# Placing loads and stores in one transfer queue of a streaming-encoder step

## The chip, the cores and the metric

The kernel runs on one core of one Trainium2 chip. The metric is the device time of one execution in microseconds. Five engines work side by side, each through its own list of instructions: TensorE (PE, with its weight loads shown apart as PEld), VectorE (DVE), ScalarE (ACT), GpSimd (POOL) and SyncE (SP). SP computes nothing here. It issues every transfer of the kernel.

## The reference, cut to what matters

One layer of an encoder with two attention branches, for 2048 new frames of one stream ("prompt") and 16 new frames of each of 8 running streams ("sample", 128 rows in all, with caches of 512 past positions):

```
h, gate = rms_norm(x) * (1 + scale) + shift, gate      # scale, shift, gate = c @ w_ada + b_ada
qa ka va za qb kb vb zb ga gb = split(h @ w_in)        # 4 heads A of 2x64, 8 heads B of 64, two gates of 1024
qa, ka = rope(qa), rope(ka)
oa = (softmax(qa1 ka1') - lam * softmax(qa2 ka2')) va  # a query sees keys of its 64-frame chunk and before
ob = stick_breaking(qb kb') vb                         # a running product over the keys, last key first
oa = rms_norm(oa) * 0.8
y  = (sigmoid(ga) * ((oa*silu(za)) @ w_a) + sigmoid(gb) * ((ob*silu(zb)) @ w_b)) @ w_out
out = rms_norm(x + gate * y)
```

The new rows of ka, va, kb and vb are outputs as well, and so are stored row by row while the projection runs.

## The kernel before

**Stages.** A first stage makes the modulated h, turns it so that features lie on partitions, splits it into a float16 high and low part, and writes it to DRAM (hT_d, 512 KB for each tile of 128 rows). The middle stage works through eight units. A unit is one head of the softmax branch (kind 0) or two heads of the stick-breaking branch (kind 1), in turn. For each unit it projects 17 tiles of h, the sample tile first, and runs causal attention for the 16 prompt tiles. A last stage does the sample attention against the caches, the branch products, the merge and the output. Between the stages o (attention output), z and the two gates g pass through DRAM (o_d, z_d, g_d).

**One step of the projection** (`project`, L405) is one tile t of one unit. Its pieces are given out one at a time: pieces 0 to 11 are two products each, 24 products over 512 columns that add up q, k, v and z in one PSUM bank (`mm`, L423 to L426: high with high, high with low, low with high, for 8 blocks of features). The piece after the last product copies the bank out on ACT to `pr` (L440), rotates q and k on POOL for kind 0 (`rot`, L459 to L464, with the small table `rope`), splits v, k and q into float16 pairs, and issues the stores: new k (L474), new v (L475), z (L477). Units 1 to 7 also carry columns of the gates, in 24 more products (L493) into the bank tagged "t", copied to one half of the buffer `gts` (L496) and stored (L497).

**Where h comes from.** `fetch_h` (L400) loads a tile of hT_d into one of three 512 KB buffers `hs`, in turn (L403). `projection` (L847) calls it for the next step at piece 2 of the running one (`H_AT`). The first tiles are at hand from the first stage.

**Attention.** `scores` multiplies q with k (L628, L629). Kind 0 takes the softmax, kind 1 a scan on DVE (L605) and a product on POOL (L611). `turn` then makes float16 pairs (L561, L562, or L289 with L294) and a transposing transfer turns them (L569) into `wt`, five buffers. Two rounds later `pv` multiplies `wt` with v (L676 to L681); ACT or DVE scales the result into `o` (L657, L663) and `store` sends it to o_d (L670).

**What sets the order.** All pieces of all projection steps stand in one list, `line`. In each round n of the middle stage (L1202) a stretch of that list, the score pieces of tile n and the pv pieces of round n - 2 are mixed by `interleave` (L91); `position` keeps the projection about five steps ahead. This gives the order in which the program is written. The framework's scheduler then decides the order on each engine: with `schedule_with_timeline_sim=True` it takes instructions on a time line of its own, and may write a transfer down earlier or later among SP's entries than it was given. On the chip each engine runs its list in that order. SP's list is one queue: an entry that has to wait holds all entries behind it. A transfer's completion is counted on one of eight semaphores, in turn.

`load` is `nc.sync.dma_start`; stores go through it too. `tc.add_manual_dep(..., NOSYNC)` binds only the written order, and adds no wait on the chip.

Of the kernel before, what the change touches and what calls it, by code (L numbers as in the profile page):

```python
# [25 lines left out]
P = 128  # L26
D = 1024
KT = D // P
# [20 lines left out]
S_TILES = 13  # L49
S_PERIOD = 6  # L50
H_AT = 2
Q_BUFS = 6
TR_AFTER = 5
LEAD = 5.0
# [55 lines left out]
def layer_kernel(ctx: ExitStack, tc: tile.TileContext, a: dict):  # L110
    nc = tc.nc
    V, S, G, T = nc.vector, nc.scalar, nc.gpsimd, nc.tensor
    load = nc.sync.dma_start
# [3 lines left out]
    def act(**kw):  # L117

        i = S.activation(**kw)  # L119
        if last_table[0] is not None:  # L120
            tc.add_manual_dep(i.ins, last_table[0].ins.name, NOSYNC, reason="table order")
        last_table[0] = i
        return i

    x_p = a["x_prompt"][0]
    x_s = a["x_sample"].rearrange("b s d -> (b s) d")
# [271 lines left out]
    at_hand, ahead, fetched = {}, {}, []  # L398

    def fetch_h(u, t):  # L400
        ahead[u, t] = hs[len(fetched) % 3].bitcast(F16).rearrange("p (f k n) -> p f k n", f=2, n=P)
        fetched.append(t)
        load(out=ahead[u, t], in_=hT_d[t // 4][:, t % 4, :, :, :])  # L403

    def project(U, t):  # L405

# [4 lines left out]
        def start():  # L411
            if t in at_hand:
                box["h"] = at_hand.pop(t)
            else:
                if (U["u"], t) not in ahead:
                    fetch_h(U["u"], t)
                box["h"] = ahead.pop((U["u"], t))
            box["p"] = bank("mm")
            if kind == 0:
                box["r"] = stg.tile([P, 96], F32, tag="rope", name="rope")  # L420
                load(out=box["r"], in_=a["shapes"][:, t * 96 : t * 96 + 96])

        def mm(n):  # L423
            hi, wi = ((0, 0), (0, 1), (1, 0))[n % 3]
            k = n // 3
            T.matmul(box["p"], box["h"][:, hi, k, :], U["w"][k][:, wi, :], start=(n == 0), stop=(n == 3 * KT - 1))  # L426

        def piece(n):
            if n == 0:
# [6 lines left out]
        def finish():  # L436
            p, s2, s = box["p"], sc[:, 2:3], sq[:, 0:1]
            pr = stg.tile([P, 512], F32, tag="pr", name="pr", bufs=3)
            first = P * kind
            S.activation(out=pr[:, first:512], in_=p[:, first:512], func=AF.Identity, scale=sc[:, 1:2])  # L440

            qb = qbuf[t % len(qbuf)]
            k16 = stg.tile([P, 2, 2, 64], F16, tag="k16", name="k16")
            vt = kvp.tile([P, 2, 2, 64], F16, tag="v", name="v", bufs=V_BUFS)

            def halves(dst, src, scale):
                src = src.rearrange("p (c d) -> p c d", d=64)
                split(dst[:, :, 0, :], dst[:, :, 1, :], src, scale, S)

            def query(src, scale):  # L450
                src = src.rearrange("p (c d) -> p c d", d=64)
                S.activation(out=qb[:, 0, :, :, :], in_=src.unsqueeze(2).to_broadcast([P, 2, 2, 64]), func=AF.Identity, scale=scale)
                V.scalar_tensor_tensor(out=qb[:, 1, :, 0, :], in0=src, scalar=scale, in1=qb[:, 0, :, 0, :], op0=ALU.mult, op1=ALU.subtract)
            if kind == 0:
                cosT, sinT = box["r"][:, 0:32], box["r"][:, 32:96]
                x4 = pr[:, 0:256].rearrange("p (c f d) -> p c f d", c=4, f=2)
                rot = stg.tile([P, 256], F32, tag="rot", name="rot")
                r2 = stg.tile([P, 256], F32, tag="r2", name="r2", bufs=1)
                G.tensor_tensor(out=rot.rearrange("p (c f d) -> p c f d", c=4, f=2), in0=x4,  # L459
                                in1=cosT.unsqueeze(1).unsqueeze(1).to_broadcast([P, 4, 2, 32]), op=ALU.mult)  # L460
                G.tensor_tensor(out=r2.rearrange("p (c f d) -> p c f d", c=4, f=2), in0=x4[:, :, ::-1, :],
                                in1=sinT.rearrange("p (f d) -> p f d", f=2).unsqueeze(1).to_broadcast([P, 4, 2, 32]),
                                op=ALU.mult)
                G.tensor_tensor(out=rot, in0=rot, in1=r2, op=ALU.add)  # L464
# [9 lines left out]
            load(out=out_rows(nk, t, h * P, P), in_=rot[:, 128:256])  # L474
            load(out=out_rows(nv, t, h * P, P), in_=pr[:, 256:384])  # L475
            ui = (h + 4 * kind) * P
            load(out=z_d[t][:, ui : ui + P], in_=pr[:, 384:512])  # L477
# [8 lines left out]
        def gate_piece(n):  # L486

            if n == 0:
                box["g"] = bank("t")
            for j in range(per * n, per * n + per):  # L490
                hi, wi = ((0, 0), (0, 1), (1, 0))[j % 3]
                k = j // 3
                T.matmul(box["g"][:, 0:gw], box["h"][:, hi, k, :], U["wg"][k // per][:, k % per, wi, :], start=(j == 0), stop=(j == 3 * KT - 1))  # L493
            if per * n + per == 3 * KT:
                gt = gts[:, t % 2 * 512 : t % 2 * 512 + 512]
                S.activation(out=gt[:, 0:gw], in_=box["g"][:, 0:gw], func=AF.Identity, scale=sc[:, 6:7])  # L496
                load(out=g_d[t][:, g0 : g0 + gw], in_=gt[:, 0:gw])  # L497
# [168 lines left out]
    def store(U, t, o):  # L666
        ui = (U["h"] + 4 * U["kind"]) * P
        if U["kind"] == 0:
            sum_squares(o, P, osums[:, t, U["h"] : U["h"] + 1])
        load(out=o_d[t][:, ui : ui + P], in_=o)  # L670

    def pv_block(job, seg, po, wj, vt, first, last):

# [173 lines left out]
    def projection(m):  # L847
# [337 lines left out]
    def early_work():  # L1185
# [202 lines left out]
```

## Time and profile before

| what | value |
| --- | --- |
| runs | 2426.85 us median of 3 (2415.17 to 2428.43) |
| profiled execution | 2416.58 us; its span, first to last instruction, 2414.4 us |
| mean granted clock of TensorE | 0.954 |
| loads of h (L403) | 130, of 512 KB each |
| turning transfers (L569) into wt | 288 |
| rope loads (L421) | 68 |
| stores of k, v, z (L474, L475, L477) | 136 of each |
| stores of o (L670), of gates (L497) | 136, 119 |
| transfers that SP issues in all | 1279 plain, 332 turning |

How to read it: the span is that of one execution taken by the hardware profiler, and the runs are timed without it. A row "A <- B: 10.0, 5, 3.0" of the waits says that A stood idle 10.0 us before its instruction, in 5 pauses, the longest 3.0 us, until B let it go. A row of the time line has the start and the length in us, the engine and line, the operation, what it writes and reads, and, in brackets, the pause ahead of it. "SPq" marks SP's list; its issue of a transfer is shown as a span there, and the transfer itself lands later.

### The profile page before, as it was taken

What the parts mean: (1) busy time and instruction counts of PE and PEld (TensorE: products, weight loads), DVE (VectorE), ACT (ScalarE), POOL (GpSimd) and SP (SyncE); (2) the same over time, 40 slices, a digit from 0 to 9 for tenths busy, and PEclk for the clock granted to TensorE, in tenths of its full rate; (3) what the DMA queues carried; (4) which work ended last, traced back from release to release, by engine and by line L of the source; (5) the groups of instructions that cost most, each with busy time, mean ns of one, the idle gap of its engine ahead of it and who ended that gap; (6) DMA issues with size and microseconds to landing.
All of it is one profiled execution on the core that took longest, in us unless ns stands there. A gap on an engine that the chain in (4) does not pass through costs nothing. (4 is left out here: it accounts for less than half of the span.)

```text
span 2414.4 us, 45136 instructions
## 1 busy us (share of the span) xinstructions
PE 2129.1 (88%) x16366; PEld 1247.2 (52%) x16366; DVE 1746.9 (72%) x3668; ACT 1664.5 (69%) x3264; POOL 754.2 (31%) x607
## 2 busy tenths in 40 slices
PE   5879998899999899899988898999995688888998
PEld 2435665565665556556555555655553344444443
DVE  4868778886676788667778976657778767777754
ACT  3658788886777878566777876665777667666652
POOL 1733023453102346220124542102334333332322
PEclk7989999999999999999999999999997889999999
DMA  9668969985886998577588866756688999998521
GB/s 334 215 204 205 215 161 217 221 182 134 189 219 168 211 195 177 129 174 177 134 215 175 182 154 149 186 129 158 154 179 184 274 240 254 252 244 214 158 104 53
DMA packets 854000, 453.91 MB, mean 188 GB/s; under 512 B 539050, under 2 KB 806362, under 8 KB 853264
## 3 DMA queue, kind: packets, MB, share of 16 engines
q1 hardware_dynamic: 853776, 451.03, 75.3%
q8 instruction: 128, 2.10, 0.4%
q14 instruction: 96, 0.79, 0.1%
HBM read 249.80 MB, written 73.44 MB: 134 GB/s over the span
## 5 line engine op out<-in xcount | busy, mean ns | idle before, releaser
L611 POOL TENSOR_TENSOR sc_p<-sc_p,sc_n 128x127 f32<-128x127 f32 (+7 forms) x192 | 318.9, 1664 | 755.4 <-DVE sc_n L605 736.6
L426 PEld LDWEIGHTS <-hs 128*128 128x128 f16 x3120 | 278.9, 99 | 320.5 <-DMA hs<-hT_d 58.4
L426 PE MATMUL ps_mm<-wa,hs 128*128 128x512 f16 x1590 | 405.9, 388 | 28.3 <-DMA hs<-hT_d 28.3
L426 PE MATMUL ps_mm<-wb,hs 128*128 128x512 f16 x1530 | 391.2, 385 | 22.6 <-DMA hs<-hT_d 19.1
L493 PEld LDWEIGHTS <-hs 128*128 128x128 f16 x2856 | 275.5, 98 | 93.9 <-DVE qst L521 4.3
L605 DVE TENSOR_TENSOR_SCAN sc_n<-ps_s,sc_n,zero_t 128x512 f32<-128x512 f32 x192 | 245.6, 1279 | 48.6 <-ACT ps_s L119 42.4
L562 DVE TENSOR_TENSOR sc_n<-sc_p,sc_n 128x128 f16<-128x128 f32 (+7 forms) x192 | 232.1, 1214 | 27.8 <-ACT sc_n L561 27.3
L628 PE MATMUL ps_s<-k,qst 128*128 128x512 f16 (+3 forms) x640 | 224.8, 352 | 29.0 <-DVE sc_n L605 24.5
L493 PE MATMUL ps_t<-wb,hs 128*128 128x256 f16 (+1 forms) x1734 | 241.0, 292 | 0.7 <-DVE qst L521 0.6
L119 ACT ACTIVATE sc_p<-ps_s,usc 128x512 f32<-128x512 f32 (+3 forms) x320 | 206.1, 644 | 36.1 <-PE ps_s L629 17.8
L629 PE MATMUL ps_s<-k,qst 128*128 128x512 f16 (+3 forms) x640 | 224.1, 352 | 0.0
L119 ACT ACTIVATE ps_s<-ps_s,usc 128x512 f32<-128x512 f32 (+3 forms) x328 | 201.4, 614 | 0.0
L561 ACT CAST sc_n<-sc_p 128x128 f16<-128x128 f32 (+7 forms) x192 | 156.1, 818 | 64.3 <-POOL sc_p L611 63.9
L680 PE MATMUL ps_o<-v,wt 128*128 128x128 f16 x1088 | 156.7, 226 | 41.0 <-DMA wt<-sc_n 40.7
L1309 PE MATMUL ps_o<-wo,wb 128*128 128x512 f16 x816 | 188.9, 385 | 0.7 <-ACT wb L1127 0.7
L1268 PE MATMUL ps_mm<-wa,wb 128*128 128x512 f16 x612 | 166.4, 403 | 20.5 <-DVE sy L225 14.2
L459 POOL TENSOR_TENSOR rot<-pr,rope 128x256 f32<-128x256 f32 x68 | 62.5, 919 | 381.6 <-ACT pr L440 299.3
L547 DVE TENSOR_SCALAR_CACHE_REDUCE sc_p<-ps_s,usc 128x512 f32<-128x512 f32 (+3 forms) x160 | 106.6, 666 | 82.0 <-PE ps_s L629 58.7
L680 PEld LDWEIGHTS <-wt 128*128 128x128 f16 x1088 | 104.5, 102 | 93.3 <-DMA wt<-sc_n 53.2
L493 PE MATMUL ps_t<-wa,hs 128*128 128x256 f16 (+1 forms) x1122 | 148.7, 282 | 1.5 <-DVE qst L521 1.5
L547 DVE TENSOR_SCALAR_CACHE_REDUCE sc_n<-ps_s,usc 128x512 f32<-128x512 f32 (+3 forms) x160 | 106.6, 666 | 53.6 <-PE ps_s L629 28.4
L681 PE MATMUL ps_o<-v,wt 128*128 128x64 f16 x1088 | 144.8, 198 | 0.0
(338 smaller groups left out, 4530.7 us busy)
## 6 DMA issues: line engine op xcount, KB each, us to landing
hs<-hT_d SPq DMA_DIRECT2D x130, 512.0 KB, 4.3
wb<-g_d SPq DMA_DIRECT2D x26, 512.0 KB, 5.1
out_dram<-pr SPq DMA_DIRECT2D x204, 64.0 KB, 2.3
g_d<-gt SPq DMA_DIRECT2D x102, 128.0 KB, 3.8
wide<-in_w_ada_dram SPq DMA_DIRECT2D x12, 1024.0 KB, 8.9
wa<-in_w_in_dram SPq DMA_DIRECT2D x34, 256.0 KB, 6.2
z_d<-pr SPq DMA_DIRECT2D x136, 64.0 KB, 1.7
o_d<-o SPq DMA_DIRECT2D x136, 64.0 KB, 3.0
```

The source lines that it names most:

```text
L119: i = S.activation(**kw)
L426: T.matmul(box["p"], box["h"][:, hi, k, :], U["w"][k][:, wi, :], start=(n == 0), stop=(n == 3 * KT - 1))
L493: T.matmul(box["g"][:, 0:gw], box["h"][:, hi, k, :], U["wg"][k // per][:, k % per, wi, :], start=(j == 0), stop=(j == 3 * KT - 1))
L547: V.tensor_scalar(out=dst[:, lo : lo + n], in0=p[:, 0:n], scalar1=sc_pos, scalar2=None, op0=ALU.mult, op1=ALU.max, accum_out=job["mx"][:, ...
L562: V.tensor_tensor(out=lo, in0=src, in1=hi, op=ALU.subtract)
L605: V.tensor_tensor_scan(out=dst[:, lo : lo + n][:, ::-1], data0=src[:, 0:n][:, ::-1], data1=zero_t[:, 0:1].to_broadcast([P, n]), initial=fi ...
L611: G.tensor_tensor(out=p[:, 0:m], in0=p[:, 0:m], in1=n[:, 1 : m + 1], op=ALU.mult)
L628: T.matmul(p[:, 0:n], qst[:, c, :], kk[:, c, 0:n], start=True, stop=False)
L629: T.matmul(p[:, 0:n], qst[:, 2 + c, :], kk[:, c, 0:n], start=False, stop=not diag)
L680: T.matmul(po[:, c * P : (c + 1) * P], wt[:, wj, :], vt[:, c, :, :], start=first, stop=False)
L1268: T.matmul(pb, st["u"][:, ui * 8 + br * 4 + k, :], wb[br * 4 + k // 2 * 2 + j][:, wi, k % 2, :], start=(n == 0), stop=(n == 11))
L1309: T.matmul(po, st["y"][:, yi * 8 + k, :], wo[j * 4 + k // 2][:, wi, k % 2, :], start=(n == 0), stop=(n == 3 * KT - 1))
```

## The change

Four things change, all in the middle stage, and no arithmetic. Line numbers are those of the kernel before.

- Each product of the projection is remembered as `last_mm`. The loads of h (L403) and of rope (L421) get an order edge to the last product given so far. So in SP's list they may not be written ahead of that product's place in the scheduler's time line: the load of h for the next step behind the fourth product of the running step, the rope load behind the last product of the step before.
- The stores at L474, L475, L477, L497 and L670 are no longer given at once. They are put in a list, which is given out at piece 5 of the next projection step (`STORE_AT`), behind its tenth product, with the same order edge. When the projection has ended, the list is given out once a round.
- The halves of `gts` alternate by the count of gate tiles, not by the parity of t. (Tile 16 and tile 0, which follow each other, had the same half.)
- Before the middle stage stores are given at once, as they were.

```diff
+STORE_AT = 5
...
+    last_mm = [None]
+
+    def not_ahead(i):
+
+        if last_mm[0] is not None:
+            tc.add_manual_dep(i.ins, last_mm[0].ins.name, NOSYNC, reason="place in the queue")
+
+    stores, late_stores = [], [False]
+
+    def store_late(**kw):
+
+        if late_stores[0]:
+            stores.append(kw)
+        else:
+            load(**kw)
+
+    def give_stores(n):
+        for kw in stores[:n]:
+            not_ahead(load(**kw))
+        del stores[:n]
...
-        load(out=ahead[u, t], in_=hT_d[t // 4][:, t % 4, :, :, :])
+        not_ahead(load(out=ahead[u, t], in_=hT_d[t // 4][:, t % 4, :, :, :]))
...
-                load(out=box["r"], in_=a["shapes"][:, t * 96 : t * 96 + 96])
+                not_ahead(load(out=box["r"], in_=a["shapes"][:, t * 96 : t * 96 + 96]))
...
-            T.matmul(box["p"], box["h"][:, hi, k, :], U["w"][k][:, wi, :], start=(n == 0), stop=(n == 3 * KT - 1))
+            last_mm[0] = T.matmul(box["p"], box["h"][:, hi, k, :], U["w"][k][:, wi, :], start=(n == 0), stop=(n == 3 * KT - 1))
...
-            load(out=out_rows(nk, t, h * P, P), in_=rot[:, 128:256])
-            load(out=out_rows(nv, t, h * P, P), in_=pr[:, 256:384])
+            store_late(out=out_rows(nk, t, h * P, P), in_=rot[:, 128:256])
+            store_late(out=out_rows(nv, t, h * P, P), in_=pr[:, 256:384])
...
-                gt = gts[:, t % 2 * 512 : t % 2 * 512 + 512]
+                j = len(gated) % 2 * 512
+                gated.append(t)
+                gt = gts[:, j : j + 512]
...
+            if i == STORE_AT:
+                give_stores(len(stores))
...
+    late_stores[0] = True
     for n in range(len(steps) + PV_LAG):
...
+        m = len(stores)
         interleave(pieces, qk, (vs, V_LO, V_HI))
+        if at[0] == len(line):
+            give_stores(m)
         jobs.append(made)
+    give_stores(len(stores))
+    late_stores[0] = False
     c01.close()
```

The stores of z, of the gates and of o are changed to `store_late` in the same way.

More of the change, by code (lines that the diff above doesn't have):

```diff
@@ L397, in layer_kernel @@
         G.memset(qb[:, 1, :, 1, :], 0.0)
-    at_hand, ahead, fetched = {}, {}, []
+    at_hand, ahead, fetched, gated = {}, {}, [], []
     def fetch_h(u, t):
@@ L473, in finish @@
             nk, nv = ("ak", "av") if kind == 0 else ("bk", "bv")
-            load(out=out_rows(nk, t, h * P, P), in_=rot[:, 128:256])
-            load(out=out_rows(nv, t, h * P, P), in_=pr[:, 256:384])
+            store_late(out=out_rows(nk, t, h * P, P), in_=rot[:, 128:256])
+            store_late(out=out_rows(nv, t, h * P, P), in_=pr[:, 256:384])
             ui = (h + 4 * kind) * P
-            load(out=z_d[t][:, ui : ui + P], in_=pr[:, 384:512])
+            store_late(out=z_d[t][:, ui : ui + P], in_=pr[:, 384:512])
             U["v"][t] = vt
@@ L494, in gate_piece @@
             if per * n + per == 3 * KT:
-                gt = gts[:, t % 2 * 512 : t % 2 * 512 + 512]
+                j = len(gated) % 2 * 512
+                gated.append(t)
+                gt = gts[:, j : j + 512]
                 S.activation(out=gt[:, 0:gw], in_=box["g"][:, 0:gw], func=AF.Identity, scale=sc[:, 6:7])
-                load(out=g_d[t][:, g0 : g0 + gw], in_=gt[:, 0:gw])
+                store_late(out=g_d[t][:, g0 : g0 + gw], in_=gt[:, 0:gw])
         return [lambda n=n: piece(n) for n in range(12)] + [lambda n=n: gate_piece(n) for n in range(3 * KT // per if gw else 0)]
@@ L669, in store @@
             sum_squares(o, P, osums[:, t, U["h"] : U["h"] + 1])
-        load(out=o_d[t][:, ui : ui + P], in_=o)
+        store_late(out=o_d[t][:, ui : ui + P], in_=o)
     def pv_block(job, seg, po, wj, vt, first, last):
```

## The prediction

> **What bounds the kernel now.** I read the page's head first, then the busy time by stretches, then who waited for whom on the tensor engine, and last the same for the queue that issues all transfers.
>
> ```profile
> span 2414.4 us, 45136 instructions
> PE 2129.1 (88%) x16366; PEld 1247.2 (52%) x16366; DVE 1746.9 (72%) x3668; ACT 1664.5 (69%) x3264; POOL 754.2 (31%) x607
> core 0: us, PE busy (x) PEld busy (x) DVE busy (x) ACT busy (x) POOL busy (x), PEclk, DMA share, GB/s
> 0.00:200.00 200.00, 139.62 (x863) 73.28 (x864) 135.30 (x370) 107.07 (x224) 83.72 (x96) 0.85 0.74 245
> 200.00:1800.00 1600.00, 1481.30 (x11532) 911.51 (x11531) 1179.48 (x2382) 1177.41 (x2469) 474.08 (x385) 0.99 0.76 177
> 1800.00:2415.00 615.00, 508.19 (x3977) 262.38 (x3973) 432.09 (x919) 379.99 (x574) 196.37 (x128) 0.91 0.76 198
> ```
>
> The three stretches are, roughly, the preparation, the eight units (projection and attention together), and the output stage. The change lives in the middle one. There the tensor engine is busy 1481.30 of 1600 us, at a granted clock of 0.99, while no other engine passes 1180 us. So the stage is bound by PE and by what makes PE stand still: 1600 - 1481.30 = 118.7 us. The next view, of the same stretch, says what ended those pauses:
>
> ```profile
> PE ps_mm L426 <- DMA hs<-hT_d: 40.4, 25, 4.1
> PE ps_o L680 <- DMA wt<-sc_n: 24.5, 21, 2.9
> PE ps_o L676 <- DMA wt<-sc_n: 22.4, 19, 3.6
> PE ps_s L628 <- DVE sc_n L605: 14.5, 19, 2.6
> ```
>
> Columns are total us, times, longest. Two transfers make 40.4 + 24.5 + 22.4 = 87.3 us of the 118.7: the load of a tile of h ahead of its projection (25 pauses), and the turned weights ahead of the products with v (40 pauses). Nothing that this change does can win more in this stage than 87.3 us, 3.6% of the run. Both transfers are issued by SP, in order, so I looked at where SP itself stood, again from 200 to 1800 us:
>
> ```profile
> SPq L403 <- PE ps_t L493: 74.7, 32, 7.8
> SPq L569 <- DVE sc_n L562: 68.2, 34, 8.2
> SPq L670 <- ACT o L657: 41.6, 21, 4.9
> SPq L475 <- ACT v L289: 32.9, 26, 4.4
> SPq L474 <- ACT v L289: 32.4, 16, 5.0
> SPq L421 <- POOL r L461: 21.0, 20, 2.8
> SPq L474 <- POOL rot L464: 19.9, 21, 2.7
> SPq L497 <- ACT gt L496: 15.3, 25, 4.2
> ```
>
> L403 is the load of h waiting until its buffer's last reader (the gate's product, L493) is done; L474, L475, L670 and L497 are stores waiting for their data; L421 is the small load of rope factors; L569 is the turning transfer, and its waits are for its own data. Stores make 41.6 + 32.9 + 32.4 + 19.9 + 15.3 = 142.1 us of standing, loads of h 74.7 us, rope 21.0 us. While SP stands at one of these, a turning transfer behind it may be ready. That is what the change is about.
>
> **What one late load looks like.** First SP's list, then PE's:
>
> ```profile
> 1197.46 0.54 SPq L670 DMA_DIRECT2D o_d<-o  x1
> 1198.05 0.42 SPq L474 DMA_DIRECT2D out_dram<-pr  x1
> 1198.58 1.21 SPq L569 DMA_TRANSPOSE wt<-sc_n  x1
> 1199.84 0.57 SPq L475 DMA_DIRECT2D out_dram<-pr  x1
> 1200.46 0.42 SPq L477 DMA_DIRECT2D z_d<-pr  x1
> 1200.98 0.38 SPq L403 DMA_DIRECT2D hs<-hT_d  x1
> 1204.72 1.47 PE L426 MATMUL ps_mm<-wa,hs 128*128 128x512 f16 x6 [1.81 <-DMA hs<-hT_d]
> ```
>
> The load went out at 1200.98 and PE went on at 1204.72, after a pause of 1.81 us. Three stores and a turning transfer stand directly ahead of it, back to back. They are not waiting here: they are being issued. Prices of such entries, min/median/max in ns, with the landing times below them in us (median):
>
> ```profile
> L403 SPq DMA_DIRECT2D hs<-hT_d x130: 319/382/2542, 139.7 to 1759.0; - x130
> L569 SPq DMA_TRANSPOSE wt<-sc_n x288: 1167/1639/6136, 158.9 to 1854.8; - x144
> L475 SPq DMA_DIRECT2D out_dram<-pr x136: 337/425/3866, 59.3 to 1793.6; - x136
> hs<-hT_d SPq DMA_DIRECT2D x130, 512.0 KB, 4.3
> wt<-sc_n SPq DMA_TRANSPOSE x288, 4.3
> 716.17 2.78 PE L493 MATMUL ps_t<-wb,hs 128*128 128x256 f16 x24
> L493 PE MATMUL ps_t<-wb,hs x1734: 272/273/421, 263.3 to 1796.5; 128*128 128x256 f16 x159, 128*128 128x512 f16 x34
> ```
>
> The last two rows give PE's pace: 24 products over 256 columns in 2.78 us, of which the last one's own 0.273 us is taken off; 23 steps of 0.109 us, or 0.00042 us a column.
>
> **The change, part by part.** No product, no activation and no transfer is added or removed: both built programs have the same instructions on every engine, 130 loads of h and 288 turning transfers among them. What differs is the order that the scheduler writes down, on SP and, as a consequence, on the other engines too (about a quarter of PE's runs of products change places). So the price is in places, and I count places in the two orders.
>
> *Stores later.* A store now follows the tenth product of the next projection instead of standing wherever its data was expected. That is less than a step: between the instruction that a store of pr waits for and the store itself stood products for 1.8 us of PE (median), now 3.1; for o 1.3, now 1.6; for the gate's rows 1.1, now 1.3. Stores of pr with no wait left of their own: 77 of 204, now 118. So the 142.1 us shrink. What that is worth I worked out from SP's list in the trace: each entry keeps its own issue time and the wait for its own data, and only the stores' waits are struck out. The loads of h then go out 0.09 us earlier on average and the turning transfers 0.08 us; cut to the pauses that PE really made, 1.5 us of 40.4 and 3.6 us of 46.9 (24.5 + 22.4) disappear. The waits at stores mostly stood in time in which nothing ready was behind them. **Term: -5.1 us.** If the waits of h and rope loads went too, the same working gives -16.2 us; if stores took no place in the queue at all, -35.7 us. Those are the bounds above zero gain; I take -5.1 because the median room of an h load, below, hardly grows.
>
> *Loads of h behind the products given.* The buffer of a load comes free at the last gate product two steps back, which the scheduler runs inside the step in between; the new bound (the fourth product of the running step) lies only a little behind that. Between release and load stood products for 2.8 us, now 3.2 (medians), for a quarter of the loads over 3.8, now 4.5. This takes from the 74.7 us of SP's standing, but it also takes from the time in which the load must land. I measured that time as the PE work (at 0.00042 us a column) between the latest product that the load or anything ahead of it on SP depends on, and the first product that reads it. In the program before, 29 of 120 loads have under 6 us, 12 have 6 to 7, 79 more; the 40.4 us fall on them as 32.2, 5.1 and 3.1. In the changed program the classes hold 34, 13 and 75. At the same loss per load (1.11, 0.43, 0.04 us) that makes 37.8 + 5.6 + 2.9 = 46.3. **Term: +5.9 us.**
>
> *Turning transfers.* Counted alike. For the softmax heads (L676) under 7 us: 8, now 6; 7 to 9: 33, now 28; more: 49, now 56; the 22.4 us become 19.3. **Term: -3.1 us.** For the stick-breaking heads (L680) under 8: 22, now 27; 8 to 12: 74, now 73; more: 79, now 76; the 24.5 us become 26.2. **Term: +1.7 us.**
>
> *Buffers held longer.* pr, rot, o and gt are freed when their store has landed. For the copies into pr at least 11 us of products lie between the store ahead and the reuse in either program; for the gate's half buffers the least rises from 5.2 to 12.7 us, because the halves now alternate by count. For o the least stays 2.2 us. Against a landing of 2 to 4 us I cost this at nothing; the cover is PE's own products, and without it each o would cost up to a landing.
>
> *Outside the stage.* In the first 200 us the stores are still given at once. After 1800 us the entries are those of before. Term: 0 us, with reordering of a few us either way.
>
> **Sum:** -5.1 + 5.9 - 3.1 + 1.7 = -0.6 us. The profiled execution took 2416.58 us (2414.4 us span and 2.2 around it), 10.3 us under the median of the runs, 2426.85. The difference is carried to the median: 2426.85 - 0.6, or **2426.2 us**.
>
> One rule speaks against even the first term. The Trainium skill, Perfetto Trace Analysis, section What "DMA-bound" means, counts as a bound the issuing engine's sequencer when its track is solid with transfers, for then the time is that of making descriptors. By that rule the waits taken away would be filled by issue work, and the sum would be -0.6 + 5.1 = +4.5 us. The trace does not bear it out here: 288 turning transfers at 1.639 us are 472 us of the 1600, and some 660 stores at 0.425 us another 280, so the track is about half full, not solid.
>
> **The rivals.** *The loads of h come too late* (slower). For: for loads with over 12 us, the entries between release and load rise from 0.70 to 1.28 turning transfers, and these wait for VectorE, up to 8.2 us at a time (L569 above); a load that stood early in the queue was safe from them. And 47 loads now have under 7 us, against 41, with a landing of 4.3. Against: for the loads under 6 us the stores ahead fall from 1.14 to 0.67 each, the turning transfers only rise from 0.24 to 0.30. Price: one more turning transfer ahead of a tight load costs 1.639 us; with half of the 47 that is 38 us, 2465 us. It passes 0.5% (12 us) from eight loads on.
>
> *The queue was worth more than my striking-out shows* (faster). Removing a wait also moves what VectorE and ACT do next, so one advance feeds another. For: 142.1 + 74.7 + 21.0 us of standing, and the order of turning transfers follows its data a little sooner (median 1.7 us of products, now 1.5). Against: for 18 of the 40 pauses at turning transfers SP issued as soon as the data was there. Price: the -35.7 us of a queue without stores, 2391 us.
>
> *The change does not do what it says*: the scheduler had most entries near these places already. That gives the forecast's time again, and so does a cancelling of terms.
>
> **How the numbers follow.** A measurement of this kernel tells about 0.5% (12 us) from no change; the three runs before span 13 us. Terms of 2 to 6 us cancel, so the likeliest single case is no difference: 0.37. The two rivals are each fed by the reordering of a quarter of PE's list, which no count here prices; the late loads get 0.36, since the count of tight loads points that way, and the freer queue 0.27. Range: from one rival's price to the other's, 2391 to 2465; beyond each I leave about 0.1. The likeliest case's own range is 2415 to 2439.
>
> **What would show it.** Waits of SP at stores should fall well under 142.1 us and those at h loads under 74.7, while the waits at L569 grow. PE's pauses at h near 46 us and at turned weights near 45 mean my terms hold. Pauses at h over 70 us: the first rival. Both sums under 60 us together: the second. If PE's busy time or the other stretches move by over 10 us, the reordering, not the queue, decided.

## The result and the profile after

| | before | changed |
| --- | --- | --- |
| median of 5 runs, us | 2426.39 (2415.17 to 2428.43) | 2444.07 (2440.44 to 2449.48) |
| ratio to before, 95% interval | 1 | 1.0085 (1.0058 to 1.0112) |
| profiled execution, us | 2416.58 | 2449.48 |
| mean granted clock in it | 0.954 | 0.946 |

The change costs 0.85%, 18 us. The two profiled executions lie 33 us apart, since that of before was a short one of its kind and that of the changed kernel a long one. In the runs of this study one kernel's time falls by about 1.1 us for each 0.001 of mean granted clock (within kernels, all runs pooled); at one clock, 0.951, before stands at 2426 us and the changed kernel at 2444. So the 18 us are real, and some 15 us of the 33 are not the change. The changed kernel lies outside the 2415 to 2439 us that the prediction gave its likeliest case.

The lines named here are 22 to 24 higher in the changed kernel than in before: L403 is L425, L493 L515, L605 L629, L628 L652, L676 L700, L680 L704, L569 L593. The late stores all appear under L144, the `load` in `give_stores`. The last gate product of the projection ends at 1825 us instead of 1797, so I read the middle stage from 200 to 1830 us against 200 to 1800 before. Busy time and the four largest waits of TensorE there:

```profile
span 2447.7 us, 45085 instructions
PE 2147.8 (88%) x16366; PEld 1251.7 (51%) x16366; DVE 1752.8 (72%) x3668; ACT 1663.5 (68%) x3264; POOL 745.1 (30%) x607
```

```profile
200.00:1830.00 1630.00, 1499.16 (x11548) 916.95 (x11546) 1186.31 (x2387) 1181.67 (x2476) 470.53 (x386) 0.97 0.76 174
```

```profile
PE ps_mm L448 <- DMA hs<-hT_d: 44.2, 27, 6.3
PE ps_s L652 <- DVE sc_n L629: 26.8, 26, 3.1
PE ps_o L700 <- DMA wt<-sc_n: 23.6, 21, 2.9
PE ps_o L704 <- DMA wt<-sc_n: 21.1, 18, 2.9
```

TensorE stands idle 1630 - 1499.16 = 130.8 us, 12.1 more than before. Loads of h and turned weights together make 44.2 + 23.6 + 21.1 = 88.9 us, against 87.3: nearly nothing. What has grown is the wait that no part of the change was aimed at, that of the score products (L652) for a PSUM bank that VectorE's scan (L629) has not yet read: 14.5 to 26.8 us (24.5 to 36.0 over the whole run). That is as much as the idle time has grown by. (The other 18 us between the stretches are TensorE busier, with the same products, at a granted clock of 0.97 instead of 0.99; most of that probably belongs to the 33 us and not to the 18.)

And SP in the same stretch:

```profile
SPq L593 <- DVE sc_n L586: 92.0, 39, 6.8
SPq L425 <- PE ps_t L515: 77.1, 30, 11.1
SPq L593 <- DVE sc_n L629: 56.3, 27, 4.8
SPq L144 <- ACT o L681: 54.6, 24, 7.3
SPq L144 <- ACT v L311: 35.7, 24, 5.8
SPq L144 <- POOL rot L486: 33.9, 18, 4.9
SPq L144 <- ACT gt L520: 30.7, 25, 3.8
```

The four large waits at stores are 54.6 + 35.7 + 33.9 + 30.7 = 154.9 us (the five of before: 142.1), that at h 77.1 (74.7). Over all rows of the stretch, small ones too, SP's waits at stores are 220.1 us before and 213.1 after, those at loads of h 96.6 and 109.3, those at turning transfers 479 and 521. So SP stands about as long as before at just what was moved. Only the waits at rope loads are gone: 24.6 us in the trace of before, 1.2 now.

**Where the scan gets late.** I went back from each of TensorE's pauses at L652 to what had released the scan. In before the scan was mostly held by VectorE's own queue: between 200 and 1830 us the scan itself had stood for ScalarE ahead of three pauses, of 0.55 us or less, and ScalarE had not stood at a load. In the changed kernel it had stood for ScalarE ahead of seven, 9.5 us together. Two of these, 5.2 us, come straight after ScalarE stood 3.8 and 3.7 us at a load that it needed for another task; in a third, 0.6 us, it had stood at a load of the projection's weights; the other four follow waits for POOL or VectorE. One of the two, first on SP, then on ScalarE, VectorE and TensorE:

```profile
830.60 1.08 SPq L144 DMA_DIRECT2D o_d<-o  x1
831.78 0.89 SPq L144 DMA_DIRECT2D out_dram<-pr  x2
832.76 1.48 SPq L593 DMA_TRANSPOSE wt<-sc_n  x1
834.29 1.14 SPq L144 DMA_DIRECT2D z_d<-pr  x1
835.48 0.43 SPq L852 DMA_DIRECT2D wb<-in_cache_a_v_dram  x1
```

```profile
840.03 1.06 ACT L293 ACTIVATE junk<-wb 128x1024 f16<-128x1024 f32 x1 [3.81 <-DMA wb<-in_cache_a_v_dram]
841.00 0.19 ACT L293 ACTIVATION_READ_ACCUMULATOR junk<-wb 128x1 f32 x1
841.09 0.67 ACT L120 ACTIVATE sc_p<-ps_s,usc 128x512 f32<-128x512 f32 x1
841.66 0.65 ACT L120 ACTIVATE ps_s<-ps_s,usc 128x512 f32<-128x512 f32 x1
```

```profile
842.34 1.22 DVE L629 TENSOR_TENSOR_SCAN sc_n<-ps_s,zero_t 128x512 f32<-128x512 f32 x1 [4.20 <-ACT ps_s L120]
```

```profile
843.61 0.38 PE L652 MATMUL ps_s<-k,qst 128*128 128x512 f16 x1 [2.67 <-DVE sc_n L629]
```

L852 (L828 of before) is a load that nothing so far has named. Beside the units the middle stage takes norms of the caches and the output weights: 80 tiles are loaded one after the other, and ScalarE adds up their squares (`junk`, L293), for use in the last stage:

```python
        def one(src, dst, scale):
            st = free.pop(0)
            free.append(st)
            load(out=st if len(src.shape) == 2 else st.rearrange("p (j n) -> p j n", n=P), in_=src)
            sum_squares(st, 1024, dst, scale=scale)
```

Nobody needs these sums soon. But ScalarE runs its list in order. Four stores and a turning transfer go out ahead of the load, it is issued at 835.48 and is there at 839.95; ScalarE stands 3.81 us at its sum; the sigmoids of the scores (L120) behind it run so much later; VectorE stands 4.20 us for them; TensorE 2.67 us for VectorE. The theory that I tested is this: **late stores and loads push the norm loads back in SP's list, and ScalarE carries the delay to the score bank.** Its first rival was that the scheduler's new order on the engines did it, a second that any new order costs something, a third that the waits only collect at the norms and would fall elsewhere without them.

### The profile page after: what moved, and what is told of

Its sections match the earlier page's. It is cut to its first block, busy times and chain, and to the rows that moved or that the text cites. A ratio compares the mean times of both kernels' runs of the same rounds, so it can differ in the third digit from the quotient of the medians.

```text
span 2447.7 us, 45085 instructions
## 1 busy us (share of the span) xinstructions
PE 2147.8 (88%) x16366; PEld 1251.7 (51%) x16366; DVE 1752.8 (72%) x3668; ACT 1663.5 (68%) x3264; POOL 745.1 (30%) x607
## 5 line engine op out<-in xcount | busy, mean ns | idle before, releaser
L635 POOL TENSOR_TENSOR sc_p<-sc_p,sc_n 128x127 f32<-128x127 f32 (+7 forms) x192 | 313.3, 1636 | 792.9 <-DVE sc_n L629 786.7
L448 PEld LDWEIGHTS <-hs 128*128 128x128 f16 x3120 | 284.2, 100 | 337.5 <-DMA hs<-hT_d 60.0
L448 PE MATMUL ps_mm<-wa,hs 128*128 128x512 f16 x1590 | 405.9, 390 | 25.7 <-DMA hs<-hT_d 25.6
L515 PEld LDWEIGHTS <-hs 128*128 128x128 f16 x2856 | 276.9, 98 | 97.7 <-issue 4.5
L629 DVE TENSOR_TENSOR_SCAN sc_n<-ps_s,sc_n,zero_t 128x512 f32<-128x512 f32 x192 | 245.4, 1278 | 48.9 <-ACT ps_s L120 43.3
L652 PE MATMUL ps_s<-k,qst 128*128 128x512 f16 (+3 forms) x640 | 226.2, 354 | 42.0 <-DVE sc_n L629 36.0
L586 DVE TENSOR_TENSOR sc_n<-sc_p,sc_n 128x128 f16<-128x128 f32 (+7 forms) x192 | 238.6, 1250 | 29.7 <-ACT sc_n L585 29.4
L515 PE MATMUL ps_t<-wb,hs 128*128 128x256 f16 (+1 forms) x1734 | 243.2, 293 | 0.4 <-DVE qst L545 0.3
L120 ACT ACTIVATE sc_p<-ps_s,usc 128x512 f32<-128x512 f32 (+3 forms) x320 | 207.8, 649 | 41.4 <-PE ps_s L656 23.5
L120 ACT ACTIVATE ps_s<-ps_s,usc 128x512 f32<-128x512 f32 (+3 forms) x328 | 203.0, 619 | 0.0
L1300 PE MATMUL ps_mm<-wa,wb 128*128 128x512 f16 x612 | 167.2, 407 | 23.4 <-DVE sc_e L245 14.8
L704 PE MATMUL ps_o<-v,wt 128*128 128x128 f16 x1088 | 153.6, 226 | 38.8 <-DMA wt<-sc_n 38.7
L515 PE MATMUL ps_t<-wa,hs 128*128 128x256 f16 (+1 forms) x1122 | 150.9, 286 | 1.7 <-DVE qst L545 1.5
L704 PEld LDWEIGHTS <-wt 128*128 128x128 f16 x1088 | 104.0, 102 | 86.5 <-DMA wt<-sc_n 50.5
L1300 PEld LDWEIGHTS <-wb 128*128 128x128 f16 x816 | 81.0, 103 | 124.5 <-issue 44.2
```

Source lines behind the costliest of these rows:

```text
L448: last_mm[0] = T.matmul(box["p"], box["h"][:, hi, k, :], U["w"][k][:, wi, :], start=(n == 0), stop=(n == 3 * KT - 1))
L586: V.tensor_tensor(out=lo, in0=src, in1=hi, op=ALU.subtract)
L629: V.tensor_tensor_scan(out=dst[:, lo : lo + n][:, ::-1], data0=src[:, 0:n][:, ::-1], data1=zero_t[:, 0:1].to_broadcast([P, n]), initial=fi ...
L635: G.tensor_tensor(out=p[:, 0:m], in0=p[:, 0:m], in1=n[:, 1 : m + 1], op=ALU.mult)
L652: T.matmul(p[:, 0:n], qst[:, c, :], kk[:, c, 0:n], start=True, stop=False)
L704: T.matmul(po[:, c * P : (c + 1) * P], wt[:, wj, :], vt[:, c, :, :], start=first, stop=False)
```

## The experiments

All times are medians of 5 to 12 runs, ratios go to runs of before on the same chip. The last column is ScalarE's waits of over 2 us for a transfer at `junk`, between 200 and 1830 us, counted in the trace. It also holds the sums over the projection's weights (loads at L343 of the changed kernel), which are not among the 80; they are all that is left in the rows of the sums_free kernels. Of the two trace columns, the one headed scan is TensorE's wait for the scan over the whole run, from its row.

| kernel | us | ratio (95%) | scan, us | at sums, us |
| --- | --- | --- | --- | --- |
| before | 2426.39 | 1 | 24.5 | 14.8 |
| changed | 2444.07 | 1.0085 (1.0058 to 1.0112) | 36.0 | 30.9 |
| queue_alone | 2442.68 | 1.0068 (1.0048 to 1.0089) | 49.2 | 48.9 |
| engines_alone | 2438.12 | 1.0054 (1.0035 to 1.0074) | 30.2 | 28.5 |
| h_alone | 2430.75 | 1.0020 (1.0005 to 1.0036) | 26.9 | 21.2 |
| stores_alone | 2436.21 | 1.0051 (1.0035 to 1.0066) | 40.7 | 35.3 |
| before_sums_free | 2423.53 | 0.9984 (0.9967 to 1.0001) | 24.7 | 6.2 |
| after_sums_free | 2430.51 | 1.0019 (0.9999 to 1.0039) | 29.4 | 13.7 |
| queue_sums_free | 2446.65 | 1.0075 (1.0051 to 1.0100) | 35.6 | 21.0 |
| stores_sums_free | 2425.91 | 0.9999 (0.9982 to 1.0015) | 34.2 | 6.1 |
| h_sums_free | 2426.16 | 0.9997 (0.9979 to 1.0016) | 27.4 | 6.8 |
| rope_only | 2431.11 | 1.0015 (0.9998 to 1.0031) | 34.0 | 16.8 |
| one_edge | 2418.14 | 0.9972 (0.9954 to 0.9990) | 22.4 | 16.7 |
| store_at8 | 2440.60 | 1.0059 (1.0037 to 1.0082) | 24.8 | 19.3 |
| at8_sums_free | 2434.71 | 1.0040 (1.0022 to 1.0058) | 23.9 | 10.6 |
| norms_late2 | 2454.83 | 1.0116 (1.0088 to 1.0144) | 40.8 | 60.2 |
| norms_late4 | 2503.55 | 1.0312 (1.0280 to 1.0343) | 79.3 | 113.1 |

The column of long waits hides one thing. Counted in all lengths, ScalarE's waits at the 80 norm sums add up to no more in the changed kernel than in before: 25.6 against 26.1 us (with the projection's weights 38.5 against 34.0). They are fewer and longer: 11 instead of 17, and those of over 2 us make 20.8 us of the 80's, against 10.9. So it isn't the sum of ScalarE's standing that grew, but its long stands. As for the places, counted by the projection's products ahead of them: 18 of the 80 norm loads go out at least 8 products later than in before, both in the changed kernel and in stores_alone; in h_alone it is 10.

### The queue's list or the engines' lists

The written order of an engine can be fixed entry by entry with the same kind of edge that the change uses. `order` below is the list of one kernel laid over the instructions of the other:

```diff
+        for a, b in zip(order, order[1:]):
+            tc.add_manual_dep(b, a.name, NOSYNC, reason='written order')
```

*queue_alone*: the changed kernel, with PE, DVE, ACT and POOL in the order of before; SP's list is the changed one, as far as these lists allow; in the traces 322 of its 1611 entries stand elsewhere than in the changed kernel, and 310 elsewhere than in before.

> The changed kernel, with the written order of PE, DVE, ACT and POOL held to that of the kernel before; only SP's list keeps the change (310 of 1611 entries stand elsewhere than before). Theory A (the loss comes from the new order on the compute engines, above all score products that wait for the scan): within 0.5% of before, 2415 to 2438 us, pauses of PE at the scan near 14.5 us. Rival B (the loss comes from the places in SP's list): 2438 us or more, as the changed kernel.

*engines_alone*: before, with the four engines in the changed order. SP's list can't stay as it was there either.

> The kernel before, without the change, with the written order of PE, DVE, ACT and POOL held to that of the changed kernel; SP's list is the scheduler's own for it (317 entries elsewhere than before). Theory A: slower by 0.5 to 1.1%, 2438 to 2453 us, pauses of PE at the scan over 20 us. Rival B: within 0.5% of before.

Measured: 2442.68 and 2438.12 us. A new order of the engines (theory A as it stood then) isn't needed for the loss, since in queue_alone the four engines run in the order of before, entry for entry, and SP's list costs 0.68% without it. Whether a new order of the engines costs something too is not shown: engines_alone moved some 316 entries of SP's list along with it. The halves don't add up to the whole (0.68 + 0.54 against 0.85%): each list here meets a partner that it wasn't worked out with. What queue_alone gave was a clear picture. Its four longest pauses for the scan, 9.0 us at 389 us among them, all had ScalarE at a sum of squares ahead, 7 to 9 us at a time: three at one of the 80 norm loads, the fourth, at 923 us, at a load of the projection's weights. That is how I came to look at `norms`.

### The two parts of the change

*stores_alone* has the late stores (the first edit, at all five stores, with the halves of `gts` by count) and leaves the loads as they were; *h_alone* has the edges of the loads of h and rope (the second edit) and gives the stores at once:

```diff
-            load(out=out_rows(nk, t, h * P, P), in_=rot[:, 128:256])
+            store_late(out=out_rows(nk, t, h * P, P), in_=rot[:, 128:256])
```

```diff
-        load(out=ahead[u, t], in_=hT_d[t // 4][:, t % 4, :, :, :])
+        not_ahead(load(out=ahead[u, t], in_=hT_d[t // 4][:, t % 4, :, :, :]))
```

> Only the loads of h and rope keep the order edge; stores are given at once and the halves of the gate buffer go by the parity of t. Orders on the engines are the scheduler's (1368 of 16246 products moved). Theory A: no telling from the edit, anything within 1% of before, and what PE's waits at the scan gain or lose is what the time does. Rival B: if loads of h are the cause, 2438 us or more with pauses at h over 45 us; if stores are, within 0.5%.

> Only the stores are given out a step later; loads of h and rope carry no order edge. Orders on the engines are the scheduler's (2415 products moved). Theory A: anything within 1% of before, following PE's waits at the scan. Rival B: 2438 us or more if stores are the cause, within 0.5% if loads of h are.

Measured: 2430.75 and 2436.21 us, 0.20 and 0.51%, together about the whole. Neither part gains anything. The larger part of the loss comes with the stores, and with them the scan's 40.7 us.

### ScalarE no longer stands at the norms' sums

The sums read a constant tile in place of the loaded one, and all five lists are fixed as they stand in the kernel that is tested, so that no entry moves. Loads, sums and their length stay (1.06 us a sum). What is lost is the value of these norms, so these kernels leave a part of the computation out. The edit also lets the next norm load go without waiting for the sum that read its tile; these waits of SP were 8.2 us in the changed kernel and 8.1 in before, so that before_sums_free is the control for them as well.

```diff
-            sum_squares(st, 1024, dst, scale=scale)
+            junk = tiny.tile([P, 1024], F16, tag="junk", name="junk", bufs=1)
+            S.activation(out=junk.rearrange("p (j n) -> p j n", n=P), in_=ident.unsqueeze(1).to_broadcast([P, 8, P]), func=AF.Square, scale=scale, accum_out=dst)
```

> The changed kernel with every engine's list and SP's list entry for entry as they are; only the 80 sums of squares of the weights' and caches' norms (L852's loads) read a constant tile in place of the tile that was loaded, so that ScalarE never stands for these loads. The norms of the caches and output weights are so left out of what is computed; loads, sums and their lengths stay. Theory (loads of the norms stand behind late stores and turning transfers in SP's list, ScalarE stands for them at its sum, the sigmoids behind it and the scan come late, TensorE pauses at the score bank): between 200 and 1830 us TensorE's waits for the scan fall from 26.8 to 14-18 us, ScalarE's waits of over 2 us at the sums from 30.9 us to nothing, and the time from 2444 to 2430-2436. Rival (the new order of the score products and the other transfers' places cost the time, the norms only fill it): the scan's waits stay at 24 or more and the time within 4 us of 2444.

> The same edit on the kernel that has the changed list of SP and the four compute engines' lists of before, again with no entry moved; the same norms are left out. Theory: this kernel's largest pauses at the score bank (9.0, 6.6, 5.1 and 4.9 us) all had ScalarE standing at such a sum ahead of them; TensorE's waits for the scan over the whole run fall from 49.2 to 25-30 us and the time from 2442.7 by 15 to 25 us, to within 6 us of the run with the same edit on before. Rival: the scan's waits stay over 40 and the time over 2437.

> The same edit on the kernel before, no entry of any list moved; the same norms are left out. The control: what standing at the sums cost there already. Both theories: its pauses for the scan had no such sum ahead of them, so that 21 us of waits for the scan stay, and the time is 2420-2426; a fall of over 8 us would say that the edit helps by something other than what separates the kernels, and only the differences between the three would count.

> The kernel with the late stores alone, no entry of any list moved; only the 80 sums of squares of the norms read a constant tile, so that ScalarE doesn't stand for the norm loads (the norms of the caches and output weights are left out). Theory (late stores stand ahead of the norm loads in SP's list, ScalarE stands at its sums, TensorE at the score bank): the stores part's 2436 falls by 8 to 14 us, TensorE's waits for the scan between 200 and 1830 us from 32.4 to 18-23. Rival (the waits only move to the turned weights and h, as when the same edit was made on the pair of changed queue and old engines' lists): the scan's waits fall but the waits for the turned weights (52.8) rise by as much, and the time stays at 2433-2439.

> The same edit on the kernel with the late loads of h and of the rotation table alone, no entry moved; the same norms are left out. Theory: its pauses for the scan (21.3 us, as before's) were hardly due to ScalarE at the sums, so that little comes off: 2427-2432. A fall of 8 us or more would say that the sums bear the loss of this part too.

Measured: the changed kernel goes from 2444.07 to 2430.51 (13.6 us), stores_alone from 2436.21 to 2425.91 (10.3), h_alone from 2430.75 to 2426.16 (4.6), and the control, before, from 2425.22 in the runs beside it to 2423.53 (1.7 by the medians; 3.9 by the ratio of 0.9984). With the control taken off, standing at the norms' sums bears 10 to 12 of the changed kernel's 18 us, and the spread of the runs leaves some 6 us either way on that. It bears most of the loss of the stores, some 7 to 9 us of 10. For the loads of h it isn't shown: 4.6 us is under the 8 that were to say so, and hardly more than the control.

The waits fell less than the theory had them fall. Between 200 and 1830 us the scan's went from 26.8 to 23.5 us in the changed kernel, where 14 to 18 were expected, and from 32.4 to 26.3 in the one with the stores alone (18 to 23). ScalarE's long waits didn't go to nothing either: 13.7 us are left at the projection's weights, which the edit does not touch.

And queue_alone stayed where it was, 2446.65. Its scan waits fell, to 35.6 us and not to the 25 to 30 that were expected, and others took their place. First queue_alone, then the same without the stands at the 80 sums:

```profile
PE ps_s L652 <- DVE sc_n L629: 49.2, 30, 9.0
PE ps_o L704 <- DMA wt<-sc_n: 42.7, 30, 4.5
PE ps_mm L448 <- DMA hs<-hT_d: 32.3, 18, 6.3
```

```profile
PE ps_o L704 <- DMA wt<-sc_n: 54.3, 28, 6.2
PE ps_s L652 <- DVE sc_n L629: 35.6, 28, 7.7
PE ps_mm L448 <- DMA hs<-hT_d: 34.6, 16, 6.3
```

13.6 us less at the scan, 11.6 more at the turned weights. The longest pause that is left at the scan, 7.7 us, is the one at the projection's weights, which the edit left in place:

```profile
921.47 1.06 ACT L293 ACTIVATE junk<-wb 128x1024 f16<-128x1024 f32 x1 [9.82 <-DMA wb<-in_w_in_dram]
925.11 0.37 PE L652 MATMUL ps_s<-k,qst 128*128 128x256 f16 x1 [7.71 <-DVE sc_n L629]
```

So this run tested the theory in part only. The turning transfers too seem to come late in this pair of lists, which were not made for each other, and to have been covered by the longer wait before. The rival of the migrating waits holds here; in the kernels whose lists belong together the time did fall. In the changed kernel too a part moves: without the stands its waits are

```profile
PE ps_mm L448 <- DMA hs<-hT_d: 57.9, 30, 6.5
PE ps_o L704 <- DMA wt<-sc_n: 36.5, 26, 4.6
PE ps_s L652 <- DVE sc_n L629: 29.4, 34, 3.1
```

over the whole run, against 50.5, 38.7 and 36.0 with them. In the idle time of this one profiled execution (2438.92 us, 8 above its own median) the gain of 13.6 us therefore isn't seen in full; it stands on the runs.

### Is a new order bad by itself?

*rope_only* places the rope loads alone behind the products, *one_edge* a single one of them:

```diff
+                rope = load(out=box["r"], in_=a["shapes"][:, t * 96 : t * 96 + 96])
+                if h == 1 and t == 1:
+                    not_ahead(rope)
```

> The kernel before with one part of the change alone: the loads of the rotation table (L421) are placed behind the products given so far; loads of h and stores as in before. SP's 24.6 us of standing ahead of these loads should fall to about 1. If SP's standing is what the time hangs on, 5 to 15 us come off. Theory: SP's standing there cost nothing, and what the time does depends on where the unedged norm loads fall; 2420-2436, unlike nothing by less than 0.5%.

> The kernel before with the edge on a single load of the rotation table (unit 1, tile 1) out of 64: nothing that the change wants is changed, but the planner, which works out its order from there on, moves 707 of TensorE's 16246 products, 144 of ScalarE's entries and 86 of SP's. If any new order of this size costs some tenths of a per cent, as with the rotation table's edges as a whole (2431), this one lies at 2428-2432; if only the kind of edge counts, at 2423-2427 as before.

Measured: 2431.11 us, not told from before, though SP's rope waits are gone; and 2418.14 us, 0.28% *faster* than before, which neither of the expected ranges held. One edge on one small load makes the scheduler write 707 of 16246 products elsewhere, and the outcome is the best kernel of the study, better than both. So the order that the scheduler happens on can be worth some tenths of a per cent, and a new one isn't bad by itself. That it can cost as much is not shown: the interval of rope_only (0.9998 to 1.0031) holds no change at all. Its waits, over the whole run:

```profile
PE ps_mm L435 <- DMA hs<-hT_d: 45.1, 26, 7.0
PE ps_o L689 <- DMA wt<-sc_n: 41.7, 31, 4.3
PE ps_o L685 <- DMA wt<-sc_n: 29.0, 25, 3.6
PE ps_s L637 <- DVE sc_n L614: 22.4, 27, 2.6
```

Against before (47.4, 40.7, 25.0, 24.5) they don't say where the 7 us come from; that stays open, and the edge has no meaning that I could defend.

### The stores at another place

```diff
-STORE_AT = 5
+STORE_AT = 8
```

> The changed kernel with the stores given out at piece 8 of a step of the projection instead of 5 (the planner moves 2298 of TensorE's products against the changed kernel). If what the stores delay is one certain place in the step, the time changes with the piece by 5 us or more, with ScalarE's waits of over 2 us at the sums (30.9 us in the changed kernel) in the same sense; if lateness as such costs, it stays within 4 us of 2444.

> The changed kernel with stores at piece 8, no entry of any list moved, only the 80 sums of squares of the norms read a constant tile (the norms of the caches and output weights are left out). Its ScalarE stood 19.3 us in waits of over 2 us at the sums, near before's 14.8, and its TensorE waited 74 us for turned weights and 48 for h. If the sums bear the loss in every order, the time falls from 2440.6 by 8 us or more; if here the turned weights and h bear it, as their waits say, it falls by 0 to 5.

Measured: 2440.60 us, within 4 of the changed kernel, but by another way. Whole run:

```profile
PE ps_o L704 <- DMA wt<-sc_n: 57.6, 35, 4.7
PE ps_mm L448 <- DMA hs<-hT_d: 54.1, 30, 6.3
PE ps_s L652 <- DVE sc_n L629: 24.8, 35, 2.0
```

The scan's wait is before's. By these rows the turned weights (both rows together 76.0 us, 65.7 before) and h (47.4 before) carry the loss. Without ScalarE's stands the time falls by 5.9 us, between the two expectations, to 2434.71, and the control's own fall of 1.7 to 3.9 us is in that. So the sums are the main channel of the kernel as it was changed, but not of every kernel with late stores. My reading, which no run here isolates: whatever stands behind the stores in SP's list comes late, and which of those transfers is tight depends on the order.

### Late norm loads, and nothing else

The last pair goes the other way. Before, complete, with all engines' lists fixed; in SP's list alone the 80 norm loads are written 2 (or up to 4) entries later. (In the traces all 80 stand behind 2 entries more in norms_late2; in norms_late4 78 stand behind 4 more, one behind 3 and one behind 2. All other entries keep their order.)

> The same with 2 entries. Theory: between before and the run with 4 entries, 2427-2440; rival: 2421-2430.

> The kernel before with every entry of the four compute engines' lists in its place and nothing left out; in SP's list 79 of the 80 norm loads stand 3 or 4 entries later, as late stores ahead of them would put them, and the entries that they let pass come so much earlier. Theory: ScalarE's waits of over 2 us at the sums rise from 14.8 us to 40 or more, TensorE's waits for the scan between 200 and 1830 us from 21 to 30-45, and the time by 8 to 25 us to 2433-2450. Rival (the norms only collect waits that would fall elsewhere; other places in SP's list cost): the transfers that are let past gain as much, and the time stays at 2421-2430.

Measured: 2454.83 and 2503.55 us. Two places in the queue cost 1.2%, where 2427 to 2440 us were expected; four places cost 3.1%, more than three times the most that I had expected. Waits of TensorE with four, over the whole run, and of ScalarE in the middle stage:

```profile
PE ps_s L628 <- DVE sc_n L605: 79.3, 46, 15.2
PE ps_o L680 <- DMA wt<-sc_n: 38.8, 30, 4.7
PE ps_mm L426 <- DMA hs<-hT_d: 33.1, 21, 6.8
```

```profile
ACT junk L271 <- DMA wa<-in_cache_a_k_dram: 32.7, 5, 8.6
ACT junk L271 <- DMA wb<-in_cache_a_v_dram: 21.5, 3, 9.7
ACT junk L271 <- DMA wb<-in_cache_b_v_dram: 16.9, 3, 7.9
...
ACT junk L271 <- DMA wa<-in_w_in_dram: 1.4, 2, 1.0
```

ScalarE's stands at the sums rise by 35 us (from 34.0 to 69.3, all lengths) and 84 us (to 118.1), the time by 30 and 79: nearly one to one. The scan's row has 16 and 55 us of that. At h 14 us came back (47.4 to 33.1), at the turned weights nothing (65.7 to 68.9). This settles that late norm loads make such a loss by themselves, and the rows put most of it, with four entries, on ScalarE and the scan. It does not say how much of the changed kernel's loss is theirs; that rests on the sums_free pairs.

## Why the prediction was wrong

**What bounds the stage.** Right: TensorE and its pauses.

**"So the 142.1 us shrink."** This failed: the large rows are 154.9 us, and all rows at stores together 213.1 against 220.1. The loads of h, which were to fall below 74.7, wait 77.1. The count of products between a store's data and the store did grow, but SP stood at the new places about as long. What was struck out of the trace of before was not what the chip did with the new list. Only the rope waits went, and rope_only, where they are gone as well, is no faster than before.

**The terms.** Their sum was near: 46.3 us foreseen at h, 44.2 measured; 45.5 at turned weights, 44.7 measured; together 1.6 us more than before. That is partly luck. At h the sign held (+3.8 for +5.9). The two terms of the turned weights had the wrong signs and cancelled: +1.2 us where -3.1 was foreseen (L676) and -3.4 where +1.7 was (L680). The -5.1 us of shorter waits of SP did not come about. (The classes of h loads also count 120 before and 122 after, a slip of at most 2.2 us.)

**"No product, no activation and no transfer is added … I count places in the two orders."** This is the step that broke. I counted places for h and turned weights, the two transfers that TensorE waits for itself. Of the other entries behind the moved ones, the 80 norm loads above all, I priced none, because no row of TensorE names them. They reach TensorE over ScalarE and VectorE, in the fourth row that I had quoted (14.5 us at the scan) and given no term. That row grew by 12.3 us. With ScalarE's stands at the norms taken out, 10 to 12 of the 18 us go.

**"Which no count here prices."** The reordering got no term, only chances. one_edge puts it at -7 us for 707 of TensorE's products moved; rope_only's +6 us, for some 1470, is not told from nothing. So it can be as large as each of my terms.

**"Outside the stage."** Nearly right: from the last product with turned weights to the end the profiled executions take 553.5 us before and 558.3 after, and 551 to 562 in the other kernels.

**The rivals.** The late loads of h (2465 us) had the right sign but not the mechanism: no rise to 70 us. The freer queue didn't come about. That the change would do nothing is out as well: 464 of SP's 1611 entries stand elsewhere.

**The test by busy time.** "If PE's busy time or the other stretches move by over 10 us, the reordering, not the queue, decided" misled. The busy time of the stretch moved by 17.9 us, which fits the lower granted clock of the one execution (0.97 for 0.99), and queue_alone shows that the queue can cost as much without any reordering of the engines.

**What stays open.** 6 to 8 of the 18 us: without the stands the changed kernel is still 7 us above before with the same edit. The waits point to h (57.9 against 49.3 us), and to sums that the edit left alone: ScalarE stands 17.5 us at the projection's weights, against 9.4 in before_sums_free. No run isolates either. What the new order of the engines costs by itself, and the loss that the loads of h bring alone, stay open too, and so does why the same queue with the old lists loses as much with turned weights as it loses with norms. Norm loads that go out *earlier* were not run; some of them already wait in SP's list for the last reader of their tile.

## What to carry to other kernels

Before moving anything in an in-order queue, list all that stands behind it, not only what the bounding engine waits for, and follow each one to the engine that stands for it: a transfer that nobody needs soon is harmless only as long as no in-order engine meets its use early. Background work in such lists is probably best placed as far behind its loads as its buffers allow; no run here tried it. Where a scheduler rewrites the order after each edit, size that effect first with an edit that means nothing, as one_edge does, before reading tenths of a per cent as the worth of an idea.

## What the runs showed of the hardware

**The granted clock falls after a long pause.** Around the 15.2 us pause of norms_late4, in windows (length, busy time and count of each engine, then granted clock, DMA share, GB/s):

```profile
380.00:388.00 8.00, 8.00 (x53) 4.88 (x52) 2.90 (x5) 1.82 (x5) 2.47 (x1) 1.00 0.86 173
388.00:404.00 16.00, 0.76 (x11) 0.52 (x10) 3.57 (x6) 7.42 (x16) 0.00 (x0) 0.62 0.41 107
404.00:408.00 4.00, 4.00 (x39) 3.33 (x38) 2.90 (x4) 1.12 (x2) 2.00 (x1) 0.50 0.59 163
408.00:412.00 4.00, 4.00 (x31) 3.05 (x30) 0.95 (x1) 2.56 (x5) 0.00 (x0) 0.89 0.02 5
```

TensorE comes back at half its clock for 4 us, and is at 0.89 in the next 4, so by these two windows the pause costs an estimated 2.4 us more than its length. The same is seen after a pause of 6.3 us in the changed kernel, 0.50 and then 0.77. The Trainium skill, TensorE: Matmul & The Clock Gate, section HAM oscillation, states it as a rule against idle gaps of over about 3.4 us; these windows agree with it. By their trace norms_late4 has 9 pauses over 3.4 us between 200 and 1830 us (63 us), queue_alone 6 (36 us), before 3 (11 us), and the mean clocks of their runs, 0.937, 0.946 and 0.952, are in that order. It isn't so for all kernels: one_edge has 4 (14.5 us) and 0.954. The changed kernel has 2 such pauses (10 us), fewer than before, so that the loss isn't explained in this way.
